# Projections of z, v and q by couples as seven block products, with more intermediates in DRAM and the last roots on ScalarE

## The chip, the cores and the metric

One core of a Trainium2 chip runs the kernel. The metric is the device time of one execution in microseconds; a profiled execution is shown by its span, which leaves out a little at both ends.

## The reference

One layer of an encoder block on x of 1024 tokens x 1024 features, float32:

```python
proj = h @ w_in                                    # 1024 x 2760
qkv, z, a, b, cq, ckv, k_rope = split(proj)
out_a = gated_deltanet(qkv, z, a, b, ...)          # conv of 4 taps + silu on q, k, v; chunked delta rule, 4 heads
out_b = mla(cq, ckv, k_rope, ...)                  # low-rank queries and keys, rotary key, block-causal softmax
h = layernorm(ALPHA * h + concat(out_a, out_b) @ w_out)
ffn = (silu(gate) * up) @ w_down                   # gate, up = causal conv of 3 taps over h @ w_up, 2 x 2816
ple = sigmoid(h @ w_gate + b) * (p @ w_proj)
out = layernorm(ALPHA * h + ffn + ple)
```

q, k, v, z are four tiles of 128 features each; the latent ckv has two and cq three; `rab` holds the rotary key and a, b. The causal convolution acts along the tokens, so a tile's second half of tokens needs the last three of its first half.

## The kernel before, in words

Every float32 product is made of three matmuls in TensorE's faster float32 format: operands are split into a high part (a copy on ScalarE) and a low part (a subtraction, mostly on DVE), and high x high, low x high and high x low are accumulated in PSUM. A projection tile is one job: `run_job` takes two halves of 512 tokens, each with `mm3` over 8 blocks of 128 features, so 48 matmuls of 128x512. `prepare_job` loads and splits a tile's weights two jobs ahead. Jobs run in the order rab, k0 to k3, v0 to v3, z0 to z3, q0 to q3, ckv, cq.

After a job `conv_half` runs the four taps (one ScalarE activation, three DVE operations that read PSUM) and a SiLU; `post_vq` and `post_z` store v, q and z to DRAM. Beside the projections run, as small generators: the gates (`gates`, ending in the `cum` matmuls), the decay matrices (`decay`, with `gg` products on POOL and DVE and `tp` matmuls), the squares and products of keys (`key_products`), the solve of 32 x 32 triangles on POOL (`solve`, 62 operations), the inverses (`inverse`, small matmuls), and the scan over eight chunks of tokens (`chunk`, `step`, `chunk_out`), which begins when v, q, z and all inverses are done. The remaining latent projections fill TensorE beside the scan. Then follow attention, the output projection, the FFN, and last `down_last`.

The order of TensorE, ScalarE, DVE and the SP queue in this part is written by a planner inside the program: each operation is booked with an assumed cost (`Engine`, a fixed time and a rate), generators yield until their inputs are booked as ready, and the order that results is pinned. POOL is booked but not pinned. Each engine then executes its list in order and waits for what it needs on the chip. Tiles come from pools with fixed counts of buffers (`s` 46, `gt` 17, `gp` 10, `raw`, `whi` and `wlo` 3 each).

The FFN up-projection, the gate and the down-projection already use seven products of half blocks in place of eight; z, v, q and the rest of `w_in` don't.

`down_last` ends the kernel: for each of eight rows of 128 tokens it adds the last products, forms mean and variance, and scales. Rows 0 to 6 take the inverse root on POOL (`inverse_root` with `e=pool`: a first guess by integer arithmetic and three Newton steps on 128x1), the last row on DVE; row 6 is finished by ScalarE and POOL.

Of the kernel before, what the change touches and what calls it, by code (L numbers as in the profile page):

```python
# [17 lines left out]
P = 128  # L18
# [20 lines left out]
ROWS = 1  # L39
RSD = 7  # L40
# [11 lines left out]
SOLVED = 15.0  # L52
# [19 lines left out]
def hybrid_block_kernel(  # L72
# [35 lines left out]
    busy, ready, used, writer = {}, {}, {}, {}  # L108
# [51 lines left out]
    class Engine:  # L160
# [5 lines left out]
        def __getattr__(self, name):  # L166
            f = getattr(self.engine, name)

            def call(*a, **k):
# [7 lines left out]
                if name == "dma_start":  # L177
                    end = book(self.engine, 0.5, 0.0, [], ins_ + outs)
# [10 lines left out]
    pool = Engine(nc.gpsimd, 0.15, 0.0019, False)  # L189

# [132 lines left out]
    matr = SR("matr", [P, 3, P])  # L323
# [13 lines left out]

    w_in_v = w_in[0].rearrange("(k p) f -> p k f", p=P)
    jobs = [("rab", [(O_KR, 64), (O_A, 8)])]
    jobs += [(f"k{h}", [((4 + h) * P, P)]) for h in range(NH)]  # L340
    jobs += [(f"v{h}", [((8 + h) * P, P)]) for h in range(NH)]
    jobs += [(f"z{h}", [(O_Z + h * P, P)]) for h in range(NH)]
    jobs += [(f"q{h}", [(h * P, P)]) for h in range(NH)]
    jobs += [(f"ckv{f}", [(O_CKV + f * P, P)]) for f in range(2)]
    jobs += [(f"cq{f}", [(O_CQ + f * P, P)]) for f in range(3)]
    w_of = [[] for _ in jobs]

    def prepare_job(j):
# [23 lines left out]

    xh = [[None, None] for _ in range(NKT)]
    xl = [[None, None] for _ in range(NKT)]

    def split_x(hf, k, ps):
        xh[k][hf], xl[k][hf] = SR(f"xh{k}{hf}"), SR(f"xl{k}{hf}")
        split(xh[k][hf], xl[k][hf], ps)

# [4 lines left out]
    for _ in range(8):  # L384
        mm(ps1[:, 0:P], junk, junk)
    def transpose_xq(i):
# [6 lines left out]
    def lower_half():  # L393
        yield wait(*xq[0])
        transpose_xq(0)
        for k in range(4):
            split_x(0, k, pieces[k])

# [10 lines left out]
    def second_half():  # L409
        yield wait(*xr)  # L410
        for k in range(NKT):
            ps = (B, G)[k % 2](f"xT1{k}")
# [29 lines left out]
    def run_job(j, post):  # L442
        ps = A(jobs[j][0])
        for hf in range(2):
            if hf == 0 and j + 2 < len(jobs) and j > 0:
                spawn(prepare_job(j + 2))
            run_half(j, ps, hf)
        for hf in range(2):
            post(hf, ps)
# [6 lines left out]
    krr = [S("krr0", [64, 512]), S("krr1", [64, 512])]  # L456
    abT = [S("abT0", [8, 512]), S("abT1", [8, 512])]
    done = set()

    def post_rab(hf, ps):  # L460
        c = slice(hf * 512, hf * 512 + 512)
        act.copy(abT[hf], ps[64:72, c])
        act.copy(krr[hf], ps[0:64, c])
# [41 lines left out]
    et_d = tc.dram_tile([NTB, P, 512], F32, name="et_d")  # L505
    qv_d = tc.dram_tile([3, NH, P, SEQ], F32, name="qv_d")
    l_d = tc.dram_tile([NTB, NH, P * P], F32, name="l_d")
    tb_d = tc.dram_tile([P, 1024], F32, name="tb_d")
    ub_d = tc.dram_tile([P, 1024], F32, name="ub_d")

# [13 lines left out]
    def conv_half(f, y, ps, hf, then):  # L524

        taps = [vec1[:, (3 - i) * 12 + f:(3 - i) * 12 + f + 1] for i in range(4)]
        act.activation(y, ps[:, hf * 512:hf * 512 + 512], AF.Identity, scale=taps[0])
        yield wait(y)
        for i in range(1, 4):
            lo_t = i if hf == 0 else 0  # L530
            d, s = y[:, lo_t:512], ps[:, hf * 512 + lo_t - i:hf * 512 + 512 - i]
            dve.scalar_tensor_tensor(d, s, taps[i], d, op0=ALU.mult, op1=ALU.add)
            yield wait(y)
        while "decay" not in done:
            yield 0.5
        act.activation(y, y, AF.Silu)
        yield wait(y)
        yield from then()
# [7 lines left out]
    flat = lambda v: v.rearrange("p t h -> p (t h)")  # L546

    def post_k(h):
        def post(hf, ps):
            def then():  # L550
                done.add(f"k{h}{hf}")
                yield 0
            spawn(conv_half(4 + h, kt[h][hf], ps, hf, then))
        return post

    l_pairs = [sbuf("gp", [P, 2, 512], f"l{j}") for j in range(NTB // 2)]
    lms = [l_pairs[t // 2][:, t % 2] for t in range(NTB)]
    ees = {}

    def decay(t):  # L560
        gg = [HR(f"gg{t}{i}") for i in range(2)]
# [3 lines left out]
        yield max(wait(*gg, maskr), room(tag))  # L565
# [4 lines left out]
        ees[t] = H(f"ee{t}")  # L570
        act.activation(ees[t], tp, AF.Exp)

    def decays():
# [3 lines left out]
        for t in range(NTB):  # L577
            spawn(decay(t), 1.3 * t)
        while len(ees) < NTB:
            yield 0.5  # L580
        done.add("decay")
        for t in range(NTB):
            yield max(wait(ees[t]), room("GB"[t % 2]))
            ep = (G, B)[t % 2](f"etp{t}")
            for h in range(NH):
                tr(ep[:, hs[h]], ees[t][:, hs[h]], ident)
            et = H(f"et{t}")
            act.copy(et, ep)
            yield wait(et)
            sync.dma_start(out=et_d[t], in_=et)  # L590
            yield 1.0
        done.add("decay_out")
        spawn(rotate_keys())

    def key_products():
        while not all(f"k{h}{hf}" in done for h in range(NH) for hf in range(2)):
            yield 0.5
        for t in range(NTB):
# [8 lines left out]
            yield wait(kd, kss)  # L607
            sync.dma_start(out=kd_d[t], in_=kd)
# [4 lines left out]
        for t in range(NTB):  # L613
            hf, c = blk[t]
            yield max(wait(bk), room("BG"[t % 2]))
            kkp = (B, G)[t % 2](f"kk_ps{t}")
            for h in range(NH):
                mm(kkp[:, hs[h]], kt[h][hf][:, c], kt[h][hf][:, c])
            lm, ee = lms[t], ees[t]
            for h in range(NH):  # L620
                dve.scalar_tensor_tensor(lm[:, hs[h]], kkp[:, hs[h]], bk[:, t, h:h + 1], ee[:, hs[h]], op0=ALU.mult, op1=ALU.mult)
            yield wait(lm)
            sync.dma_start(out=l_d[t].rearrange("h (p c) -> p h c", c=P), in_=heads(lm))
# [3 lines left out]

    whole = {}

    def solve():  # L630
# [8 lines left out]
        for j in range(31):  # L639
# [4 lines left out]
            pool.tensor_tensor(tb_[:, m:, 0:m], tb_[:, m:, 0:m], tv, op=ALU.subtract)  # L644
        yield wait(tb_)
# [4 lines left out]
        whole["tw"], whole["uw"] = [], []  # L650
        for hf in range(2):
            for name, d in (("tw", tb_d), ("uw", ub_d)):
                v = d.rearrange("(b i) (r s) -> (i r) b s", i=4, s=32)
                y = S(f"{name}{hf}", [P, 16, 32])
                sync.dma_start(out=y, in_=v[:, 16 * hf:16 * hf + 16])
                whole[name].append(y.rearrange("p (t h) s -> p t h s", h=NH))
        yield SOLVED
        for j in range(NTB // 2):
            yield from inverse(j)


    def inverse(j):

        u = l_pairs[j].rearrange("p t (h c) -> p t h c", c=P)
        tw, uw = (whole[n][j // 2][:, 2 * (j % 2):2 * (j % 2) + 2] for n in ("tw", "uw"))
# [6 lines left out]
        nw = H(f"nw{j}", [96, 2, NH, 32])  # L672
        for i in (0, 64):
            act.mul(nw[i:i + 32], pw[i:i + 32], -1.0)
        ti = H(f"ti{j}", [64, 2, NH, 64])
# [19 lines left out]
        nw2 = H(f"nw2{j}", [64, 2, NH, 64])  # L695
# [21 lines left out]
    chunks, states, outs = {}, [None], []  # L717

    def chunk(t):
# [3 lines left out]
        sync.dma_start(out=et, in_=et_d[t])  # L723
        sync.dma_start(out=kd, in_=kd_d[t])
        qc, vc = load_chunk("qc", 1, t), load_chunk("vc", 0, t)
        yield max(wait(qc, et), room("B", "G"))
        qk = B(f"qk_ps{t}")
        for h in range(NH):
            mm(qk[:, hs[h]], kt[h][hf][:, c], qc[:, hs[h]])
# [12 lines left out]
        chunks[t] = qc, et, vc, kd  # L742

    def step(t):

        hf, c = blk[t]
        while t not in chunks:
            yield 0.3
        qc, et, r, kd = chunks[t]
        state = states[t]  # L750
        if state is not None:
            yield max(wait(state, r), room("G"))
            ks = G(f"ks_ps{t}")
            for h in range(NH):
                mm(ks[:, hs[h]], kt[h][hf][:, c], state[:, hs[h]])
# [8 lines left out]
        if t < NTB - 1:  # L764
# [10 lines left out]
            states.append(new)  # L775
        spawn(chunk_out(t, qc, et, vn, state), 0.4)
# [38 lines left out]
    def scan():  # L815
        while not all(f"{n}{h}{hf}" in done for n in "vqz" for h in range(NH) for hf in range(2)) or "decay_out" not in done:
            yield 0.5
        yield wait(qv_d, et_d, kd_d)
# [3 lines left out]
        while not all(f"inverse{j}" in done for j in range(NTB // 2)):  # L822
            yield 0.5
# [3 lines left out]
    def post_vq(a, h, f):  # L827
        def post(hf, ps):
            y = S(f"{'vq'[a]}{h}_{hf}")
            def then():  # L830
                sync.dma_start(out=qv_d[a, h, :, hf * 512:hf * 512 + 512], in_=y)
                yield 0
                done.add(f"{'vq'[a]}{h}{hf}")
            spawn(conv_half(f, y, ps, hf, then))
        return post

    def post_z(h):
        def post(hf, ps):
            y = S(f"z{h}_{hf}")
            act.activation(y, ps[:, hf * 512:hf * 512 + 512], AF.Silu)  # L840
            sync.dma_start(out=qv_d[2, h, :, hf * 512:hf * 512 + 512], in_=y)
# [1120 lines left out]
```

## Time and profile before

| | |
|---|---|
| runs (3) | median 1372.06 us (1371.88 to 1374.73) |
| profiled execution | 1371.56 us, span 1369.7 us |
| granted TensorE clock, mean | 0.992 |
| PE busy | 1333.5 us (97%), 7185 matmuls |
| DVE busy | 986.3 us (72%) |
| ScalarE busy | 626.6 us (46%) |
| POOL busy | 189.2 us (14%) |

Busy matmul time is modelled and counts the pipeline, so matmuls overlap in it: what one costs in a stream is read from the distance of their starts. Stretches are given in microseconds from the span's start.

### The profile page before, as it was taken

The page shows a single profiled execution, that of the slowest core. Times are in us where ns is not written, and L with a number is a line of the kernel's source. Part 1 is how long each engine was busy: PE and PEld are TensorE (multiplying, and loading weights), DVE is VectorE, ACT ScalarE, POOL GpSimd, SP SyncE. Part 2 cuts the span into 40 slices and gives each one's busy share as a digit, 9 for nine tenths or more (in the row PEclk, how much of TensorE's full clock was granted, in tenths as well). Part 3 has the DMA queues.
Part 4 walks back from the last instruction along what each step waited for, and adds up shares of the span by engine and source line. Part 5 has one row for each costly group of instructions (what it writes and reads, how often), then busy time and mean ns, then how long its engine had stood idle before and what let it go on. Part 6 is the DMA issues. An engine that isn't in the chain of part 4 may idle for free.

```text
span 1369.7 us, 19833 instructions
## 1 busy us (share of the span) xinstructions
PE 1333.5 (97%) x7185; PEld 1127.6 (82%) x7185; DVE 986.3 (72%) x1781; ACT 626.6 (46%) x1213; POOL 189.2 (14%) x418
## 2 busy tenths in 40 slices
PE   9999999999989999999999999999999999999995
PEld 6788887789878988888998888888888888888884
DVE  3746224365467795777889888888888887988857
ACT  3544123555335572246435555555555554444511
POOL 0341450144420000230000000000000000000036
PEclk9999999999999999999999999999999999999998
DMA  7034535445431243336452221222212249406112
GB/s 219 24 119 151 139 100 132 140 121 146 108 114 58 81 127 107 120 108 214 148 162 78 85 85 63 92 93 77 92 64 91 93 164 361 160 22 205 51 44 94
DMA packets 181089, 159.19 MB, mean 116 GB/s; under 512 B 26138, under 2 KB 140672, under 8 KB 180992
## 3 DMA queue, kind: packets, MB, share of 16 engines
q1 hardware_dynamic: 180784, 157.67, 37.0%
q8 instruction: 56, 0.92, 0.3%
q14 instruction: 41, 0.34, 0.1%
q10 hardware_dynamic: 144, 0.26, 0.1%
q0 software_dynamic: 64, 0.00, 0.0%
HBM read 117.53 MB, written 39.85 MB: 115 GB/s over the span
## 4 chain that ended last, share of the span: by engine, by line
PE 54%; DVE 3%; POOL 2%; issue 1%; ACT 1%; DMA 1%; SPq 0%; DVEq 0%; ACTq 0%; POOLq 0%
PE ffX L199 17%; PE ffZ L199 9%; PE dX L199 7%; PE dP L199 5%; PE ffY L199 4%; PE gX L199 3%; PE mixp L199 3%; PE gY0P L199 1%; PE gY1P L199 1%; POOL rs_u L170 1%; DVE h L170 1%; PE dl L199 1%; POOL ln_v L170 1%; DMA mix_raw<-mm_d 1%; POOL ln_rs L170 0%
## 5 line engine op out<-in xcount | busy, mean ns | idle before, releaser
L170 POOL TENSOR_SCALAR ln_v<-ln_ss 128x1 f32<-128x1 f32 x7 | 9.0, 1285 | 710.6 <-ACT sink L170 710.1
L199 PE MATMUL dX<-dP,dP 128*128 128x512 f32 x432 | 99.5, 390 | 0.0
L199 PEld LDWEIGHTS dX<-dP,dP 128*128 128x128 f32 x432 | 81.1, 188 | 17.0 <-DVE h L170 0.2
L170 DVE SCALAR_TENSOR_TENSOR gate<-c,vec,gate 128x511 f32<-128x511 f32 (+1 forms) x132 | 69.8, 571 | 11.4 <-ACT gate L170 10.7
L199 PE MATMUL dP<-dP,dP 128*128 128x512 f32 x324 | 75.4, 391 | 0.0
L199 PEld LDWEIGHTS dP<-dP,dP 128*128 128x128 f32 x324 | 60.6, 188 | 13.3 <-DVE h L170 0.9
L170 ACT CAST dP<-b 128x512 fp32r<-128x512 f32 x45 | 28.0, 622 | 60.4 <-issue 20.8
L170 ACT COPY c<-ffX 128x512 f32<-128x512 f32 x44 | 25.8, 586 | 38.4 <-PE ffX L199 38.4
L170 ACT ACTIVATE gate<-c,vec 128x512 f32<-128x512 f32 x44 | 35.9, 817 | 14.8 <-DVE c L170 12.8
L170 DVE SCALAR_TENSOR_TENSOR u<-ffX,vec,u 128x511 f32<-128x511 f32 (+1 forms) x88 | 40.2, 478 | 0.1
L170 DVE SCALAR_TENSOR_TENSOR u<-c,vec,u 128x511 f32<-128x511 f32 (+1 forms) x44 | 33.0, 751 | 7.1 <-ACT u L170 6.3
L170 ACT ACTIVATE p<-s,mx,q_f 128x128 f32<-128x128 f32 (+7 forms) x32 | 26.7, 835 | 24.8 <-DVE mx L170 21.1
L170 DVE TENSOR_TENSOR dP<-b,dP 128x512 fp32r<-128x512 f32 x45 | 31.0, 690 | 8.5 <-ACT dP L170 8.4
L170 ACT ACTIVATE gate<-gate 128x512 f32<-128x512 f32 x44 | 27.6, 627 | 12.1 <-DVE gate L170 12.1
L199 PE MATMUL ov<-pth,v 128*128 128x256 f32 x160 | 31.3, 287 | 0.1
L170 DVE TENSOR_TENSOR dP<-a,dP 128x512 fp32r<-128x512 f32 x45 | 31.0, 688 | 0.0
L170 DVE TENSOR_TENSOR ptl<-pt,pth 128x512 fp32r<-128x512 f32 (+1 forms) x40 | 24.8, 633 | 7.9 <-ACT pth L170 7.8
L170 DVE TENSOR_TENSOR u<-u,gate 128x512 f32<-128x512 f32 x44 | 30.2, 686 | 0.0
L170 DVE SCALAR_TENSOR_TENSOR kt<-k,vec,kt 128x512 f32<-128x512 f32 (+3 forms) x24 | 16.4, 740 | 19.0 <-ACT kt L170 19.0
L170 ACT CAST dP<-a 128x512 fp32r<-128x512 f32 x45 | 27.7, 617 | 5.1 <-issue 2.2
L170 POOL TENSOR_TENSOR h<-h,b 128x1024 f32<-128x1024 f32 x8 | 19.3, 2414 | 76.4 <-DVE h L170 75.1
L170 ACT ACTIVATE u<-ffX,vec 128x512 f32<-128x512 f32 x22 | 17.2, 780 | 23.1 <-PE ffX L199 23.1
(1373 smaller groups left out, 4179.5 us busy)
## 6 DMA issues: line engine op xcount, KB each, us to landing
wup<-in_ffn_w_up_dram SPq DMA_DIRECT2D x88, 256.0 KB
b<-in_ffn_w_down_dram SPq DMA_DIRECT2D x54, 256.0 KB
a<-g_d SPq DMA_DIRECT2D x45, 256.0 KB
g_d<-u SPq DMA_DIRECT2D x44, 256.0 KB
wgP_raw<-in_ple_w_gate_dram SPq DMA_DIRECT2D x16, 512.0 KB
wo_raw<-in_w_out_dram SPq DMA_DIRECT2D x8, 512.0 KB
xres<-in_x_dram SPq DMA_DIRECT2D x8, 512.0 KB
pp_d<-pp SPq DMA_DIRECT2D x16, 256.0 KB
```

Source lines behind the costliest of these rows:

```text
L170: ins = f(*a, **k)
L199: on_pe(nc.tensor.matmul(o, a, b, start=start, stop=stop, **k_), max((k - 1.0) * a.shape[-1] / 1900.0, n * k / 2370.0), o, a, b)
```

## The change

1. The 12 tiles of z, v and q are taken in six couples, z0 with z1 to q2 with q3. With the two tiles as blocks of columns, the two halves of the features as blocks of the sum and the two halves of the tokens, each couple is a 2 x 2 block product that is computed with seven products of 12 matmuls instead of eight. The four sums of weights per couple run on POOL; the sums of blocks of x (T1 to T4) are made once, by ScalarE copies and 24 POOL operations, and split like the others.

```diff
+    couples = [("z0", "z1"), ("z2", "z3"), ("v0", "v1"), ("v2", "v3"), ("q0", "q1"), ("q2", "q3")]
+    TERMS = {"P1": ("X", "B11"), "P2": ("Y", "B21"), "P5": ("Y", "T1"), "P6": ("X", "T2"), "P3": ("Y", "B22"), "P7": ("X", "T3"), "P4": ("X", "T4")}
...
+    def pair_operand(n):
...
+        act.copy(w[:, 0], src)
+        yield wait(w)
+        dve.tensor_tensor(w[:, 1], src, f32(w[:, 0]), op=ALU.subtract)
+        d[name] = w
+        if name == "P2":
...
+            pool.tensor_tensor(a21, a11, a21, op=ALU.subtract)
+            pool.tensor_tensor(d["s"], a22, a21, op=ALU.subtract)
+            pool.tensor_tensor(a11, d["s"], a11, op=ALU.add)
+            pool.tensor_tensor(a12, a12, d["s"], op=ALU.subtract)
+
+    def pair_operands():
+        for n in range(len(seq)):
+            while n > place[0] + 3:
+                yield 0.3
...
+        for k in range(4):
+            until(lambda: xb[block][k] is not None)
+            h, l = xb[block][k]
+            for i, (a, b) in enumerate(((0, h), (1, h), (0, l))):
+                settle(w, b)
+                mm(ps, w[:, a, k], b, start=first and k == i == 0, stop=k == 3 and i == 2, skip_group_check=not first)
```

2. The block results are combined with one ScalarE copy and one DVE addition each (`pair_after`), except the last; the taps of a tile then read SBUF (three halves of a couple) or PSUM (one), and the first three tokens of the second half are completed by three short operations (`conv_edge`). At most two tiles of v or q are in their convolution at a time.

3. More waits in DRAM: the keys after SiLU (`qv_d` gets a fourth part, and each chunk loads its own), the decay matrices with their transposes (`ee_d`), the key products until the inverse, and the split x of features 0 to 511, tokens 512 to 1023 (`b12_d`, read again for ckv and cq). Key products begin when all decays are done. The solve yields between its steps; an inverse is made per pair of chunks, and a step of the scan waits only for its own. The planner's assumed costs of ScalarE and DVE are larger in this part:

```diff
+    usual = {e: (e.fixed, e.rate) for e in (act, dve)}
+    act.fixed, act.rate, dve.fixed, dve.rate = 0.2, 0.00078, 0.16, 0.00105
...
-        while t not in chunks:
+        while t not in chunks or f"inverse{t // 2}" not in done:
...
             pool.tensor_tensor(tb_[:, m:, 0:m], tb_[:, m:, 0:m], tv, op=ALU.subtract)
+            yield 1.2
```

4. In `down_last` all roots go to ScalarE, with the first guess on DVE; all rows but the last are finished by one DVE operation.

```diff
+        def root(v, scale):
+
+            h, y = T("ln_v", 1), T("ln_rs", 1)
+            act.activation(h, v, AF.Identity, scale=-0.5 * scale, bias=eps)
+            dve.tensor_scalar(y.bitcast(I32), h.bitcast(I32), -0.5, float(0x5F3759DF - 2 ** 22 - 2 ** 30), op0=ALU.mult, op1=ALU.add)
+            for _ in range(3):
+                u, w, z = T("rs_u", 1), T("o_ms", NH)[:, 0:1], T("ln_rs", 1)
+                act.activation(u, y, AF.Identity, scale=h)
+                act.activation(w, u, AF.Identity, scale=y, bias=three)
+                act.activation(z, w, AF.Identity, scale=y)
+                y = z
+            return y
...
         def finish_row(t):
-            if t < NTB - 1 - ROWS:
-                dve.scalar_tensor_tensor(acc[t], acc[t], rss[t], b, op0=ALU.mult, op1=ALU.add)
-            else:
-                act.mul(acc[t], acc[t], rss[t])
-                pool.tensor_tensor(acc[t], acc[t], b, op=ALU.add)
+            dve.scalar_tensor_tensor(acc[t], acc[t], rss[t], b, op0=ALU.mult, op1=ALU.add)
```

## Rows read from the trace of the kernel before

**Rows 1.** The page: chain of waits, and gigabytes per second in 40 slices.

```profile
PE 54%; DVE 3%; POOL 2%; issue 1%; ACT 1%; DMA 1%; SPq 0%; DVEq 0%; ACTq 0%; POOLq 0%
...
GB/s 219 24 119 151 139 100 132 140 121 146 108 114 58 81 127 107 120 108 214 148 162 78 85 85 63 92 93 77 92 64 91 93 164 361 160 22 205 51 44 94
```

**Rows 2.** Timeline, projections: start, duration, engine, line, operation, count.

```profile
85.33 1.98 PE L199 MATMUL v<-xh,v_hi 128*128 128x512 f32 x8
87.14 1.98 PE L199 MATMUL v<-xh,v_lo 128*128 128x512 f32 x8
...
227.85 0.39 PE L199 MATMUL ckv<-xh,ckv_hi 128*128 128x512 f32 x1
```

**Rows 3.** Windows: stretch, length, PE, PEld, DVE, ACT, POOL, clock, DMA, GB/s.

```profile
85.30:227.90 142.60, 142.60 (x706) 118.98 (x704) 60.58 (x100) 45.42 (x114) 54.67 (x94) 1.00 0.47 126
153.00:194.00 41.00, 41.00 (x183) 33.97 (x182) 5.33 (x4) 7.23 (x10) 36.04 (x62) 1.00 0.40 112
...
900.00:1000.00 100.00, 100.00 (x443) 82.87 (x442) 86.48 (x150) 51.49 (x83) 0.00 (x0) 1.00 0.27 84
```

**Rows 4.** Groups of DVE by form: shapes, count, busy, mean ns, idle before.

```profile
L170 DVE TENSOR_TENSOR dP<-b,dP 128x512 fp32r<-128x512 f32 x45 | 31.0, 690 | 8.5 <-ACT dP L170 8.4
L170 DVE SCALAR_TENSOR_TENSOR u<-c,vec,u 128x511 f32<-128x511 f32 x22 | 16.5, 751 | 6.3 <-ACT u L170 6.3
...
L170 DVE SCALAR_TENSOR_TENSOR l<-kk_ps,gs,ee 128x128 f32<-128x128 f32 x32 | 9.0, 344 | 6.6 <-POOL tb__1376 L170 3.4 <-PE kk_ps L199 3.1
L170 DVE SCALAR_TENSOR_TENSOR v<-v,vec,v 128x512 f32<-128x512 f32 x12 | 8.9, 743 | 0.0
...
L170 DVE TENSOR_TENSOR v_lo<-v_raw,v_hi 128x1024 fp32r<-128x1024 f32 x4 | 4.9, 1219 | 0.6 <-ACT v_hi L170 0.6
```

**Rows 5.** Groups of POOL by form, the first 300 us.

```profile
L170 POOL TENSOR_TENSOR gg<-mats,g_hi 128x512 fp32r<-128x512 f32 x8 | 10.4, 1326 | 18.3 <-DVE g_hi L170 18.3
```

**Rows 6.** Timeline of POOL and of DVE, decays.

```profile
43.42 10.37 POOL L170 TENSOR_TENSOR gg<-mats,g_hi 128x512 fp32r<-128x512 f32 x8 [18.31 <-DVE g_hi L170]
...
45.44 1.58 DVE L170 TENSOR_TENSOR gg<-mats,g_lo 128x512 fp32r<-128x512 f32 x1
...
48.25 1.21 DVE L170 TENSOR_TENSOR gg<-mats,g_lo 128x512 fp32r<-128x512 f32 x1
49.38 2.06 DVE L170 TENSOR_TENSOR k_lo<-k_raw,k_hi 128x1024 fp32r<-128x1024 f32 x1
...
52.02 0.87 DVE L170 TENSOR_TENSOR gg<-mats,g_lo 128x512 fp32r<-128x512 f32 x1
...
53.47 3.27 DVE L170 TENSOR_TENSOR gg<-mats,g_lo 128x512 fp32r<-128x512 f32 x5
```

**Rows 7.** Timeline of DVE and of POOL, rotation of queries.

```profile
377.39 1.67 DVE L170 TENSOR_TENSOR qm<-qm,qm 128x512 f32<-128x512 f32 x1
...
378.59 1.62 POOL L170 TENSOR_TENSOR qm<-qm,qm 128x512 f32<-128x512 f32 x1
```

**Rows 8.** Timeline of PE, gates.

```profile
43.57 0.75 PE L199 MATMUL cum<-gs,mats 128*128 128x32 f32 x6
```

**Rows 9.** Timeline of PE, DVE and POOL at the end; ScalarE's smallest operation, scan.

```profile
1353.87 0.28 PE L199 MATMUL dl<-wl,gh 128*128 128x256 f32 x1
...
1354.14 1.28 DVE L170 SCALAR_TENSOR_TENSOR h<-h,ln_rs,b 128x1024 f32<-128x1024 f32 x1 [1.49 <-POOL ln_rs L170]
...
1358.78 0.41 DVE L170 TENSOR_TENSOR h<-dl,h 128x256 f32<-128x256 f32 x1
...
1361.20 2.29 DVE L170 SCALAR_TENSOR_TENSOR ln_rs<-rs_u,ln_rs 128x1 f32<-128x1 f32 x1
...
1365.08 1.41 DVE L170 SCALAR_TENSOR_TENSOR h<-h,ln_rs,b 128x512 f32<-128x512 f32 x2
...
1360.96 2.52 POOL L170 TENSOR_TENSOR h<-h,b 128x1024 f32<-128x1024 f32 x1 [1.26 <-ACT h L170]
...
249.04 0.20 ACT L170 ACTIVATE junk<-junk 128x1 f32<-128x1 f32 x1
```

More of the change, by code (lines that the diff above doesn't have):

```diff
@@ L509, in hybrid_block_kernel @@
     ub_d = tc.dram_tile([P, 1024], F32, name="ub_d")
+    drams.update(key(x[:]) for x in (kd_d, ee_d, qv_d, l_d))
     def heads(ap):
@@ L534, in conv_half, with conv_taker, take, halves @@
         while "decay" not in done:
             yield 0.5
-        act.activation(y, y, AF.Silu)
+        act.activation(y, src, AF.Silu)
         yield wait(y)
-        yield from then()
+    live = set()
+    def conv_taker(f_of, out_of, then):
+        ys = {}
+        def take(name, role, hf, c):
+            f = f_of(name)
+            def halves():
+                if name not in ys:
+                    while name[0] != "k" and len(live) > 1:
+                        yield 0.3
+                    if name not in ys:
+                        if name[0] != "k":
+                            live.add(name)
+                        ys[name] = out_of(name)
+                y = ys[name]
+                yield from conv(f, y[hf], c[hf])
+                if role == "a" and hf == 1:
+                    conv_edge(f, y[1], c[0])
+                    done.add(f"conv {name}")
+                if role == "b" and hf == 0:
+                    conv_edge(f, y[1], c[0])
+                    done.add(f"conv {name}")
+                for i in {("a", 0): (0,), ("a", 1): (1,), ("b", 1): (), ("b", 0): (0, 1)}[role, hf]:
+                    yield from silu(y[i], y[i])
+                    then(name, i, y[i])
+                    if (role, i) in (("a", 1), ("b", 1)):
+                        live.discard(name)
+            spawn(halves())
+        return take
@@ L564, in decay @@
         tag = "BG"[t % 2]
-        yield max(wait(*gg, maskr), room(tag))
+        yield max(wait(whole, maskr), room(tag))
         tp = (B, G)[t % 2](f"tp{t}")
@@ L569, in decay @@
             mm(tp, utrir, y, start=False, stop=i == 1)
-        ees[t] = H(f"ee{t}")
-        act.activation(ees[t], tp, AF.Exp)
+        ees[t] = sbuf("gp", [P, 2, 512], f"ee{t}")
+        act.activation(ees[t][:, 0], tp, AF.Exp)
+        yield max(wait(ees[t]), room("GB"[t % 2]))
+        ep = (G, B)[t % 2](f"etp{t}")
+        for h in range(NH):
+            tr(ep[:, hs[h]], ees[t][:, 0, hs[h]], ident)
+        act.copy(ees[t][:, 1], ep)
+        yield wait(ees[t])
+        sync.dma_start(out=ee_d[t], in_=ees[t])
+        done.add(f"decay{t}")
     def decays():
@@ L577, in decays, with put, load_decays @@
         for t in range(NTB):
-            spawn(decay(t), 1.3 * t)
-        while len(ees) < NTB:
-            yield 0.5
-        done.add("decay")
[L582 to L592, printed above, removed]
-        spawn(rotate_keys())
+            spawn(decay(t))
+            while t > 1 and f"decay{t - 2}" not in done:
+                yield 0.2
+        while not all(f"decay{t}" in done for t in range(NTB)):
+            yield 0.2
+        done.add("decay")
+        spawn(rotate_keys())
+    def put(kd, t):
+        yield wait(kd)
+        sync.dma_start(out=kd_d[t], in_=kd)
+    def load_decays(j):
+        y = sbuf("gp", [P, 2, 512], f"lm{j}")
+        sync.dma_start(out=y, in_=ee_d[2 * j:2 * j + 2, :, 0].rearrange("t p c -> p t c"))
+        return y
     def key_products():
-        while not all(f"k{h}{hf}" in done for h in range(NH) for hf in range(2)):
+        while not all(f"k{h}{hf}" in done for h in range(NH) for hf in range(2)) or "decay" not in done:
             yield 0.5
@@ L775, in step @@
             states.append(new)
+        done.add(f"step{t}")
         spawn(chunk_out(t, qc, et, vn, state), 0.4)
@@ L815, in scan @@
     def scan():
-        while not all(f"{n}{h}{hf}" in done for n in "vqz" for h in range(NH) for hf in range(2)) or "decay_out" not in done:
+        while not all(f"{n}{h}{hf}" in done for n in "vqz" for h in range(NH) for hf in range(2)) or "projected" not in done:
             yield 0.5
-        yield wait(qv_d, et_d, kd_d)
+        yield wait(qv_d, ee_d, kd_d)
         act.activation(junk[:, 0:1], junk[:, 0:1], AF.Exp)
@@ L821, in scan, with out_pair, keep, take_z @@
         spawn(chunk(1), 2.0)
-        while not all(f"inverse{j}" in done for j in range(NTB // 2)):
-            yield 0.5
         for t in range(NTB):
             yield from step(t)
[L827 to L841, printed above, removed]
-            done.add(f"z{h}{hf}")
-        return post
+    def out_pair(name):
+        y = sbuf("gp", [P, 2, 512], f"{name}_out")
+        return y[:, 0], y[:, 1]
+    def keep(name, hf, y):
+        sync.dma_start(out=qv_d["vqz".index(name[0]), int(name[1]), :, hf * 512:hf * 512 + 512], in_=y)
+        done.add(f"{name}{hf}")
+    takers["v"] = conv_taker(lambda name: 8 + int(name[1]), out_pair, keep)
+    takers["q"] = conv_taker(lambda name: int(name[1]), out_pair, keep)
+    def take_z(name, role, hf, c):
+        y = c[hf]
+        if role == "b" and hf == 0:
+            y = H(f"{name}_{hf}")
+            act.copy(y, c[hf])
+        def gate():
+            yield from silu(y, y)
+            keep(name, hf, y)
+        spawn(gate())
+    takers["z"] = take_z
     raws, tot = {}, {}
@@ L1035, in value_pair @@
         for t2 in range(NTB // 2):
+            if h == 0:
+                until(lambda: f"step{2 * t2 + 1}" in done)
             ps = (B, G)[t2 % 2](f"v_{h}_{t2}", [P, 2, 256])
```

422 lines of the change are left out of this document (281 added, 141 removed).

## The prediction

> **What bounds the kernel now.** I read the chain of waits on the page first: TensorE holds 54% of it, with a POOL entry for the small tiles `rs_u`, `ln_v`, `ln_rs` that can only come from the last layer norm [rows 1]. Then TensorE in order of time over the projections: the reader is to see groups of eight 128x512 matmuls that follow each other at 1.81 us without a gap, from the first v (85.33) to the first ckv matmul (227.85) [rows 2]. The busy times of that stretch agree: PE 142.6 of 142.6 us, DVE 60.6, POOL 54.7 [rows 3]. So until 228 us TensorE's count of matmuls sets the time. In the last 16 us another thing does: the last matmul ends at 1354.15, while DVE was until 1354.14 waiting for POOL's `ln_rs` and ends 11 us later [rows 9].
>
> **Removed matmuls.** Before, 12 tiles cost 2 halves x 8 x 3 = 48 matmuls each, 576. After, 6 couples cost 7 products x 4 x 3 = 84 each, 504. One is 1.81 / 8 = 0.2266 us [rows 2], so 72 x 0.2266 = **-16.3 us** if nothing else becomes late. The stretch would shrink from 142.5 to 126.2 us.
>
> **What must fit beside it on DVE.** Durations are those of rows 4: 0.69 for a two-tensor operation of 128x512, 0.75 for a convolution tap, 0.344 for a 128x128 step of the key products, 0.74 for a tap from PSUM. A couple needs 7 low parts and 3 additions, 6.9 us; a v or q couple also 12 taps (9.0) and 6 short edges, which I put at 0.15 each, 16.8 us. Two z couples are 13.8, four v/q couples 67.2; nine low parts of the sums of x 6.2, the last key tile's taps 4.4, `kd` 5.5, key products 32 x 0.344 = 11.0. Together 108.1 of 126.2 us, a slack of 18. That load alone is bearable: in the FFN, which is made of the same seven products, DVE is busy 86% while PE has no gap [rows 3].
>
> **What it shares with POOL.** The change puts 24 sums of weights on POOL in this stage, beside nine operations of the key rotation and the 62 of the solve (36.0 us [rows 3]). A 128x512 sum takes POOL about 1.3 us [rows 5], so 24 x 1.3 + 9 x 1.3 + 36 = 79 us. When POOL and DVE work on SBUF tensors at the same time they lengthen each other. Where POOL ran 8 such operations in 10.37 us, three `gg` of DVE took 1.58, 1.21 and 0.87 against 0.65 undisturbed, and `k_lo` 2.06 against 1.22 [rows 4, 6]: 2.5 us lost, 0.25 per us of POOL. Where both run nothing but such operations, one of DVE takes 1.67 instead of 0.65 beside one of 1.62 on POOL [rows 7]: 0.63 per us. Lower end: 0.25 x 79 = 20, less the slack, +2 us. Upper end: 0.63 on the 57 us that lie beside v and q couples and 0.25 on the other 22, 41 less 18, +23 us. What DVE loses beyond its slack goes to TensorE, since the low part of each operand is queued on DVE behind the taps and is made only three products (8 us) ahead. I take **+10**: DVE's mix here, with additions and some taps from PSUM, is nearer to rows 6, and some of the solve will fall behind the projections.
>
> The Trainium skill, page "SBUF — State Buffer", section "Who interferes with whom", speaks against the change here: a DVE instruction with two SBUF inputs and a GpSimd instruction that reads SBUF exclude each other, and the second waits for the whole of the first. The lengths in rows 6, 7 and 9 agree. By that rule alone the sum takes the third rival's term below in place of +10.
>
> **The start.** 24 sums of x go to POOL from about 15 us, when the lower blocks are split: 24 x 1.3 = 31 us, until 46. POOL is now idle until 43.42, when the first `gg` of the decays runs [rows 6], and `cum` on TensorE waits for the gates at 43.57 [rows 8]. The gates' own small two-tensor operations on DVE run in those microseconds, and DVE also gets seven low parts (4.8 us). Bounds: 0 if other k matmuls stand ahead of `cum` and the first `tp`, +5 if the whole overlap turns into a wait. I take **+3**: 46.4 - 43.4.
>
> **Edits that I put at nothing.** Eight extra ScalarE copies at the start, the block copies and splits later: ScalarE is busy 45 of 142.6 us [rows 3], and about 40 us more still fits; it is tight (by the same count some 45 of 49 us) only beside the z couples and the key squares. Stores and loads of keys, decays, x: some 6 MB more in 126 us, 48 GB/s on top of 126 [rows 3]; the page has slices above 300 [rows 1]. They also stand in SP's queue ahead of weight loads, and a store that waits for a late SiLU holds the next weights; with a lead of 8 us this costs only when DVE is late already. The inverse, scan and latent projections keep their matmuls; the scan may start as soon as one inverse is done, while the first values wait for its steps (their `gp` buffers) and have their weights prepared later than now. For the waits around all these I take 0, bounds -4 to +4.
>
> **The end.** Before: the last pair of `h` operations starts at 1365.08, 10.9 us after the last matmul, because finishing row 5 waited for POOL, so DVE takes the last 256 columns only at 1358.78; a step of the root then takes 2.29 us beside POOL's `h<-h,b` of 2.52 [rows 9]. After: no POOL work. DVE needs per row 2 x 0.65 + 1.3 + 1.3 + 0.2 = 4.1 us, and PE 24 x 0.2266 = 5.4, so DVE keeps up. From the last matmul: addition, statistics and aggregate 1.2, ScalarE's `h` 0.3, first guess on DVE 0.2 = 1.7. Then DVE has row 6 (1.3) and two halves (1.4), until 4.4, and ScalarE nine operations of 128x1 at 0.20 [rows 9], 3.6; if each dependent step costs 0.30, 4.5. The last pair starts at 4.5 instead of 10.9: **-6.4** (bounds -4 to -7).
>
> **Sum.** The profiled execution took 1371.56 (span 1369.7 and 1.9 around it): 1371.56 - 16.3 + 10 + 3 - 6.4 = 1361.9. The median of the runs is 0.5 above that execution: 1362.
>
> **Rivals.**
> - *Everything is covered.* POOL's sums fall beside DVE's PSUM work and PE keeps its 0.2266: 1371.56 - 16.3 - 6.4 + 0.5 = 1349. For it: the FFN's gapless TensorE at 86% DVE. Against: no POOL work lies beside the FFN.
> - *DVE and POOL alternate (the slower side).* Place: v and q couples while the solve runs. Price 0.63 on all POOL work there, plus late convolutions that hold PSUM: +36 when the slack of 18 is already used by the key products sliding out of the z couples; 1371.56 - 22.7 + 3 + 36 + 0.5 = 1388. It decides from 0.48 lost per us of POOL on (0.48 x 79 - 18 = 20 eats both gains). For: rows 7. Against: rows 6.
> - *The shared access itself is full.* DVE's two-SBUF operations, 14 + 28 + 9 low parts at 0.69 and 36 taps at 0.75, are 62 us; with POOL's 79 that is 141 in 126.2 us: +15, 1371.56 - 22.7 + 3 + 15 + 0.5 = 1367. This is the rule of the Trainium skill named above.
> - *The solve ends late.* It ran from 153 to 194; if shared POOL time moves its end by over 25 us while projections end 16 us earlier, latent projections run out before the scan does: +8 on the forecast, 1370.
> - *The roots on ScalarE don't shorten the end* (each step over 0.4 us): only POOL's block on DVE goes, 2.3 us; 1366.
>
> **How the numbers follow.** Forecast 0.38 (own range 1355 to 1368); covered 0.24; full access 0.12; alternation 0.18; late solve 0.04; end not shorter 0.04. 0.2% is 2.7 us, about what a measurement of this kernel tells from no change. Faster: 0.38 + 0.24 + 0.06 + 0.04 = 0.72; same: the rest of the full access and the late solve with a share of the alternation, 0.09; slower 0.19. The range 1348 to 1380 leaves out half of the alternation and a few hundredths below.
>
> **What would show it.** Right: 504 matmuls in the couples at 0.227, DVE above 85% beside v and q, low parts of 1 us and more while POOL runs, gaps before products that end on DVE or POOL, a last pair 4 to 5 us after the last matmul. Wrong: couples without gaps beside the solve (then 1349), or gaps of over 20 us in sum. The end is wrong if a ScalarE step takes over 0.3 us.

## The result, and the profile after

| | median of the runs | range | profiled execution |
|---|---|---|---|
| before | 1371.97 us | 1371.44 to 1374.73 (4 runs) | 1371.56, span 1369.7 |
| after | 1436.03 us | 1434.58 to 1438.35 (4 runs) | 1436.09, span 1434.3 |

The change makes the kernel slower, 1.046 times the time before (95% interval 1.0445 to 1.0475), 64 us; the forecast was 1362 us, 10 us faster. Landmarks on TensorE, us from the start of the span:

| | before | after | stage, after minus before |
|---|---|---|---|
| `cum` starts | 43.57 | 51.89 | |
| last matmul of the k tiles ends | 85.3 | 103.9 | +18.6 |
| first `ckv` matmul | 227.85 | 303.2 | +56.8 |
| first `kn` matmul | 362.05 | 431.5 | -5.9 |
| last `dl` matmul starts | 1353.87 | 1423.2 | |
| last pair of `h` operations starts, after that matmul | 11.2 | 6.5 | -4.7 |

The loss lies in two stages: the start, and above all the couples, the stage that was to shrink by 16.3 us and grow by 10. The page of the kernel after, its TensorE and clock slices and the chain, which answers to [rows 1] (there 54% PE, 1% ACT):

```profile
PE   8786877799998999999999999999999999999996
...
PEclk9987999999999999999999999999999999999999
...
PE 71%; DVE 5%; ACT 5%; issue 2%; DMA 1%; POOL 1%; SPq 0%; DVEq 0%; ACTq 0%; POOLq 0%
```

A slice is 36 us: TensorE is no longer full in the first eight. The windows of the same kernel (stretch, length, then busy time of PE, PEld, DVE, ACT, POOL, granted clock, DMA share, GB/s) answer to the first line of [rows 3], where PE was busy 142.60 of 142.60:

```profile
30.00:40.00 10.00, 8.56 (x30) 4.33 (x29) 3.06 (x6) 3.98 (x9) 9.69 (x11) 0.83 0.48 126
...
100.00:120.00 20.00, 12.34 (x42) 8.73 (x41) 14.52 (x23) 10.17 (x19) 9.90 (x8) 0.83 0.09 33
103.90:303.20 199.30, 151.04 (x682) 112.15 (x681) 113.73 (x183) 78.65 (x182) 81.64 (x112) 0.91 0.39 116
303.20:431.50 128.30, 124.54 (x1077) 108.52 (x1076) 65.77 (x142) 69.83 (x229) 40.12 (x141) 1.00 0.62 166
```

In 199.3 us TensorE is busy 151, and part of that at the lower of its two clock levels, 1.2 and 2.4 GHz (mean granted clock 0.91, before 1.00). DVE is busy 114 of 199 us: it is not full. What TensorE waited for in the couples (engine, line, releaser: sum in us, times, longest):

```profile
PE pair L198 <- DVE c L167: 17.6, 17, 3.0
PE pair L198 <- ACT c L167: 17.0, 17, 5.2
PE pair L198 <- ACT win4P L167: 6.1, 1, 6.1
PE pair L198 <- DVE win0P L167: 2.5, 1, 2.5
PE pair L198 <- ACT win0P L167: 2.4, 1, 2.4
```

34 waits are for `c`, the copies and additions that take a product out of PSUM. The third couple in order of time: the first matmuls of its products, answering to [rows 2], and below, from DVE and ScalarE, what each waited for.

```profile
190.19 0.73 PE L198 MATMUL pair<-xh,win2P 128*128 128x512 f32 x2 [0.67 <-ACT c L167]
...
193.99 0.74 PE L198 MATMUL pair<-xT2h,win2P 128*128 128x512 f32 x2 [0.78 <-DVE c L167]
...
197.72 0.73 PE L198 MATMUL pair<-xT1h,win2P 128*128 128x512 f32 x2 [0.68 <-ACT c L167]
...
201.41 0.73 PE L198 MATMUL pair<-xT3h,win2P 128*128 128x512 f32 x2 [0.68 <-ACT c L167]
```

```profile
193.24 0.69 DVE L167 TENSOR_TENSOR c<-pair,c 128x512 f32<-128x512 f32 x1 [1.86 <-PE pair L198]
...
197.08 0.58 ACT L167 COPY c<-pair 128x512 f32<-128x512 f32 x1 [1.88 <-PE pair L198]
...
200.78 0.58 ACT L167 COPY c<-pair 128x512 f32<-128x512 f32 x1 [2.06 <-PE pair L198]
```

The product that starts at 193.99 (`xT2h`, P6) adds to X. What it waits for, the addition from 193.24 to 193.93, reads Y, which P2 has just finished. The next one writes Y and waits for the copy of X. A product takes 3.7 us where twelve matmuls at 0.2266 take 2.72: the wait and some 0.25 us around it, 1.0 us each time.

### The profile page after: what moved, and what is told of

It reads as the page before. It is cut to its first block, busy times and chain, and to the rows that moved or that the text cites. A ratio compares the mean times of both kernels' runs of the same rounds, so it can differ in the third digit from the quotient of the medians.

```text
span 1434.3 us, 20071 instructions
## 1 busy us (share of the span) xinstructions
PE 1344.6 (94%) x7113; PEld 1121.9 (78%) x7113; DVE 1046.2 (73%) x1882; ACT 687.1 (48%) x1366; POOL 223.7 (16%) x389
## 4 chain that ended last, share of the span: by engine, by line
PE 71%; DVE 5%; ACT 5%; issue 2%; DMA 1%; POOL 1%; SPq 0%; DVEq 0%; ACTq 0%; POOLq 0%
PE ffX L198 17%; PE ffZ L198 8%; PE dX L198 7%; PE dP L198 5%; PE ffY L198 4%; PE mixp L198 4%; PE pair L198 4%; PE gX L198 3%; PE s L198 3%; PE cq L198 2%; PE ov L198 2%; PE ckv L198 2%; PE gY0P L198 1%; PE gY1P L198 1%; PE v L198 1%
## 5 line engine op out<-in xcount | busy, mean ns | idle before, releaser
L167 DVE TENSOR_TENSOR c<-pair,c 128x512 f32<-128x512 f32 x18 | 12.4, 690 | 35.0 <-PE pair L198 31.7
L167 ACT ACTIVATE p<-s,mx,q_f 128x128 f32<-128x128 f32 (+7 forms) x32 | 26.7, 834 | 22.3 <-DVE mx L167 18.6
L167 DVE SCALAR_TENSOR_TENSOR kt<-k,vec,kt 128x511 f32<-128x511 f32 (+5 forms) x36 | 19.0, 563 | 24.3 <-ACT kt L167 24.0
L167 ACT ACTIVATE c<-c 128x512 f32<-128x512 f32 x22 | 13.6, 630 | 30.9 <-DVE c L167 30.9
```

The lines of the kernel that those rows point to most:

```text
L167: ins = f(*a, **k)
```

## The experiments

Each was run in three rounds beside the kernel before; ratios are to it, with 95% intervals. The base of the later ones is the third.

| run | edit | us | ratio |
|---|---|---|---|
| e1 | X and Y in PSUM tiles of their own | 1404.31 | 1.0226 [1.0209, 1.0243] |
| e2 | splits of the sums of x after the decays | 1409.1 | 1.0253 [1.0228, 1.0278] |
| e3 | both | 1394.35 | 1.015 [1.0133, 1.0167] |
| e4 | the kernel before with the new end alone | 1369.21 | 0.9966 [0.9953, 0.9979] |
| e5 | e3, sums of weights on DVE | 1397.39 | 1.0175 [1.0153, 1.0197] |
| e6 | e3 without the solve's operations | 1382.06 | 1.0063 [1.0048, 1.0078] |
| e7 | e3, first couple earlier, sums of x after the gates | 1405.2 | 1.0227 [1.0207, 1.0247] |
| e8 | e5 and e7 | 1420.38 | 1.0343 [1.0327, 1.0358] |
| e9 | e3, z couples beside the solve | 1400.01 | 1.0197 [1.0175, 1.0219] |
| e10 | e3 without the sums of x | 1376.28 | 1.0023 [1.0014, 1.0032] |
| e11 | e10 and e6 | 1363.13 | 0.9922 [0.9906, 0.9939] |
| e12 | e9, copies of x by POOL | 1416.41 | 1.0311 [1.0278, 1.0344] |

**e1, X and Y apart.**

```diff
-                until(lambda: f"conv {last}" in done)
-            y = A(f"pair{f}")
-            d["X"], d["Y"] = y[:, 0:512], y[:, 512:1024]
...
+            d[bank_] = A(f"pair{bank_}{f}")[:, 0:512]
...
+            d["C21"] = H(f"c21_{f}")
+            act.copy(d["C21"], d["X"])
```

> The changed kernel, with the two chains X and Y of a couple in two PSUM tiles instead of two halves of one, and the last X copied out at once. Theory A (the shared tile makes each product wait until the one before it is taken out of PSUM): products follow each other at 2.7 instead of 3.7 to 3.9 us, the 34 us of waits for the copies and additions c nearly vanish (one per couple stays), the couples lose 35 to 50 us and the kernel comes to about 1390 to 1400. Theory B (my prediction: DVE and POOL hold each other up): the waits only move to the operands, less than 10 us are gained, 1426 or more.

-31.7 us. The same copies and additions are there, and one copy more in each couple of v and q, but the third couple of e1 runs through (its products start 2.72 us apart, with nothing named before them):

```profile
175.38 0.62 PE L198 MATMUL pairY<-xh,win2P 128*128 128x512 f32 x2
...
178.10 0.62 PE L198 MATMUL pairX<-xT2h,win2P 128*128 128x512 f32 x2
...
180.82 0.62 PE L198 MATMUL pairY<-xT1h,win2P 128*128 128x512 f32 x2
```

In the couples of e1 the waits for `c` are 2.5 us instead of 34.6. The couples lose 29.8 us (169.5 instead of 199.3) and not 35 to 50, as other waits take part of the place: those for the operands `win3P` to `win5P` rise from 8.9 to 16.0 us, and one of 4.7 for the taps of the last key tile (`kt`) comes up. The edit does one thing beside the tiles: with the last X copied out, a couple no longer waits for a convolution that still reads PSUM (the `until` above). No wait of a couple's matmul in the kernel after is for such taps, so this isn't where the 34.6 us were. So the order was kept by the tile and not by what its halves hold. The Trainium skill ("PSUM — Partial Sum Buffer", section "PSUM bank collisions raise a hardware error") asks for semaphores by bank and quadrant; X and Y are 2 KB per partition each, and here the waits went by the tile, wider than that rule.

**e2, late splits, and e3, both.**

```diff
-        yield 5.0
+        while "decay" not in done:
+            yield 0.5
         for name, m in [("T2", m) for m in range(4)] + [("T1", m) for m in range(3)]:
```

> The changed kernel, with the splits of the sums T2 and T1 of x begun only when the decays are done. Theory A (the splits fill ScalarE's and DVE's lists in front of the decays and the taps of the keys, which delays the end of the keys from 85 to 104 us): the keys end 10 to 15 us earlier, 1421 to 1426, if the first couple doesn't wait for the sums instead. Theory B (POOL's sums of x hold the gates, or the decays two at a time are slow by themselves): the keys end no more than 4 us earlier.

> Both edits together. If both theories A hold: the sum of the two gains, about 1375 to 1385. If the first couple waits for the late sums: no better than the split tiles alone.

e2 gives -27 us, more than expected. In the profiled executions, 24.2 us apart, 12.2 lie before the end of the k tiles (91.7 instead of 103.9), 7.3 in the couples and 4.9 between the first `ckv` and the first `kn` matmul. The first couple waits for its own operands as before (2.4 and 2.8 us), but the longest wait for `c` falls from 5.2 to 2.1. In the kernel after, ScalarE and DVE, which work through their lists in order, show why (ScalarE's casts wait for DVE's low parts, and the first `exp` of the decays, `ee<-tp`, stands behind them until 65.14):

```profile
53.81 0.62 ACT L167 CAST xT1h<-xT 128x512 fp32r<-128x512 f32 x1 [5.31 <-DVE xT2l L167]
...
57.66 0.62 ACT L167 CAST xT1h<-xT 128x512 fp32r<-128x512 f32 x1 [3.07 <-DVE xT2l L167]
...
62.52 0.62 ACT L167 CAST xT1h<-xT 128x512 fp32r<-128x512 f32 x1 [4.24 <-DVE xT1l L167]
...
65.14 0.59 ACT L167 ACTIVATE ee<-tp 128x512 f32<-128x512 f32 x1
```

e3 missed its 1375 to 1385. The two gains overlap: 32 and 27 alone, 42 together. Part of both is the same, as the traces read: the long waits for `c` of the first couple, and the low clock with them (from 120 to 160 us 0.74 and 0.83 in the kernel after, 0.88 and 1.00 in e1, 0.87 and 1.00 in e2).

**e4, the new end alone** (the layer norm's tail of the kernel after, put into the kernel before; everything else is before).

> The kernel before, with only its last part taken from the changed kernel (roots on ScalarE, rows finished on DVE). The end after the last matmul took 15.6 us before and 10.8 after the change, so 4.5 to 5 us less, 1367. If the gain came from elsewhere than these lines: within 1 us of 1372.

0.34% faster by the ratio, 4.7 us (interval 2.9 to 6.5), over 10 runs against 13. This is the one part of the change that pays, and the version to keep.

**e5, sums of weights on DVE; e6, no solve.** What e3 still waits for in the couples, and what e6 does:

```diff
-            pool.tensor_tensor(a21, a11, a21, op=ALU.subtract)
+            dve.tensor_tensor(a21, a11, a21, op=ALU.subtract)
...
-            pool.tensor_tensor(tv, lb[:, m:, j:j + 1].broadcast_to([P, n, m]),
-                                    tb_[:, j:j + 1, 0:m].broadcast_to([P, n, m]), op=ALU.mult)
-            pool.tensor_tensor(tb_[:, m:, 0:m], tb_[:, m:, 0:m], tv, op=ALU.subtract)
```

> The kernel with X and Y in tiles of their own and late sums of x (1394), and the four sums of weights of each couple on DVE instead of POOL. What it still loses beside the solve are waits of TensorE for the operands of the third and fourth couple: 8.3 us for a ScalarE cast, 4.7, 1.4 and 1.3 for DVE's low parts. Theory Q (the sums stand in POOL's list between the 62 operations of the solve: the second sum of a couple started 12 us after the first): these waits go, the operands come in time, 1380 to 1386. Theory L (POOL and DVE lengthen each other, as the prediction had it at +10): the sums leave POOL but add 0.7 to 1.1 us each to a DVE that is busy 18.2 to 18.7 of 20 us there; taps stay at 1.0 to 1.1 us and the waits move to DVE: 1390 to 1398.

> The same base (1394) with the 62 operations of the solve on POOL left out (its table stays the identity, so the inverse is not computed; its loads, stores and the rest stay). Both theories of the loss beside the solve agree that it goes, so this measures its size, which the prediction put at +10: waits for operands of the third and fourth couple at 0 to 2 us in place of 15, taps of DVE at 0.75 us in place of 1.0 to 1.1, and 1375 to 1383. A third theory, that ScalarE's copies are the limit of a couple: still over 1388. The scan may also start earlier or later by a few us.

Waits of TensorE, first e3, then e6:

```profile
PE pairX L198 <- ACT win4P L167: 8.3, 1, 8.3
PE pairX L198 <- DVE win3P L167: 4.7, 1, 4.7
PE pairY L198 <- DVE kt L167: 4.6, 1, 4.6
```

```profile
PE pairY L198 <- DVE kt L167: 5.7, 1, 5.7
PE pairY L198 <- ACT win5P L167: 3.9, 1, 3.9
...
PE pairX L198 <- DVE win4P L167: 2.2, 1, 2.2
...
PE pairX L198 <- DVE win3P L167: 0.7, 1, 0.7
```

Without the solve the kernel is 12.3 us shorter. Taking the sums off POOL gave nothing (+3.0): DVE, busy 18.7 of 20 us from 180 to 200 in e3, is busy 19.7 there in e5. That speaks for theory L, DVE lengthened by POOL, and against the late place in POOL's list as the whole story. One product shows both. In e3 the second sum of the fifth couple's weights (`win_s`) starts at 213.07, 13.5 us after the first, with the solve in between, and its cast on ScalarE at 218.70, behind a SiLU that waited for DVE's taps. In e5 the same sum is done at 209.95, and the product still starts only at 218.67, after 5.3 us of waiting for DVE's low part. DVE's line in e3 while the solve runs, and then in e6 without it:

```profile
191.82 1.12 DVE L167 SCALAR_TENSOR_TENSOR v_out<-c,vec,v_out 128x511 f32<-128x511 f32 x1
192.87 1.17 DVE L167 TENSOR_TENSOR win3P<-win,win3P 128x512 fp32r<-128x512 f32 x1
...
199.24 0.69 DVE L167 TENSOR_TENSOR c<-pairX,c 128x512 f32<-128x512 f32 x1
```

```profile
189.40 0.75 DVE L167 SCALAR_TENSOR_TENSOR v_out<-c,vec,v_out 128x511 f32<-128x511 f32 x1
190.06 0.69 DVE L167 TENSOR_TENSOR win3P<-win,win3P 128x512 fp32r<-128x512 f32 x1
```

Beside the solve taps and low parts take 1.1 us for the 0.75 and 0.69 of [rows 4] and of e6; the addition that reads PSUM keeps its 0.69.

**e7 and e8, the first couple earlier.**

```diff
-            if hf == 0 and j == 4:
+            if hf == 0 and j == 3:
                 load_pair(0, 0)
...
+                    act.copy(c[hf], ps[:, hf * 512:hf * 512 + 512])
...
+        while "gates" not in done:
+            yield 0.5
...
-                pool.tensor_tensor(low[o, m], low[a, m], low[b, m], op=ALU.subtract)
+            later.append((m, sums))
```

> The same base (1394) with three edits at the first couple: the 24 sums of x on POOL begin after the gates, the weights of the first couple are loaded and its first two operands split one key tile earlier, and the last key tile is copied out of PSUM by ScalarE before its taps, so that Y's tile is free. It tells what is left of the start: TensorE now waits 2.4 and 2.5 us for the first couple's operands, 4.6 for the taps of the last key tile, and works at 0.80 of its clock from 100 to 120 us. If these are late operands and a late tile, they go and with them the low clock: 1377 to 1384. If DVE's list there (late low parts of the sums of x) is the limit, another wait takes their place: 1390 to 1396.

> The edits of both: sums of weights on DVE and the early first couple. If the two losses are independent, the gains add: 1365 to 1375. If DVE's list is full, the early operands and the sums displace each other and it stays at 1380 to 1392.

Both missed: +10.9 and +26.0. The sums didn't move behind the gates: the planner doesn't pin POOL's order, and in the trace they ran without a pause from 25.9 to 56.7, over the whole of the gates, so `cum` came at 59.2. In e8 the first couple waits 8.9 us in two pieces for its last low part of x (5.6 in e7, where the weights' sums are on POOL). e8 is 8.5 us behind e3 at the first `kn` matmul, and the rest of the 26 is lost after it. There the scan runs on into attention: its last transposes (`oT_ps`) start at 438.6, in e3 at 396.4. Why the scan ends so late was not taken apart by a run.

**e9, the z couples beside the solve.**

```diff
-    couples = [("z0", "z1"), ("z2", "z3"), ("v0", "v1"), ("v2", "v3"), ("q0", "q1"), ("q2", "q3")]
+    couples = [("v0", "v1"), ("v2", "v3"), ("q0", "q1"), ("z0", "z1"), ("z2", "z3"), ("q2", "q3")]
```

> The base with X and Y apart and late sums (1394), the couples in another order: v, v, q, z, z, q in place of z, z, v, v, q, q, so that the two z couples, which put no convolution on DVE (6.9 us of it per 19 us of TensorE instead of 16.8), stand where the solve runs on POOL. Theory L (the loss beside the solve is DVE lengthened by POOL): the 15 us of waits for operands of the third and fourth couple shrink to 0 to 5, and 1380 to 1388. Theory Q (the sums of weights are late in POOL's list): the waits stay, 1390 to 1398. Against both: v couples then stand beside the key products and the last splits of x, which may cost 3 to 8 us at the first couple.

The first `ckv` matmul comes 4 us earlier (258.9 for 262.9), and the waits for operands of the fourth and fifth couple (`win3P`, `win4P`) fall from 14.3 to 7.8 us, but DVE is now busy 19.9 of 20 us from 140 to 160, and what is gained is lost again after the couples (the scan's last transposes start at 410.4 instead of 396.4): 1400, outside what either theory expected. It doesn't tell the theories apart.

**e10, no sums of x; e11, also no solve.**

```diff
-            y = low[name, m] = S(f"x{name}{m}")
-            act.copy(y, ps)
...
+        for n, b in (("T1", "B11"), ("T2", "B21"), ("T3", "B22"), ("T4", "B11")):
+            xb[n] = xb[b]
```

> The base (1394) without the sums of x: no copies of x by ScalarE at the start, no sums on POOL, no splits; the products of T1 to T4 read blocks of x that are there already, so the products have the same matmuls and wrong values. It measures what the sums of x cost from the first transposes to the last couple. Theory S (the start's loss is these sums: transposes that wait 0.5 to 1.2 us for ScalarE's copies, TensorE then at 0.5 to 0.8 of its clock from 30 to 40 us, and 128x32 operations of the gates that take 0.8 to 1.06 us beside POOL instead of 0.18): cum back at 43.5 to 45 from 53.5, the k tiles end at 85 to 87 instead of 92, waits at the first couple (2.4, 2.5, 4.6) shrink; 1378 to 1386. Rival: the start's loss is the extra decay stores and key stores on the queues: cum stays above 50, 1390 or more.

> Both left out, the sums of x and the 62 operations of the solve: what the seven products would give with POOL nearly free. If the two losses add (12 from the solve, 8 to 16 from the sums), 1364 to 1374. If the products without POOL's company ran gapless, as my rival of full cover had it, the first ckv matmul would come at 212 to 215 and the time be 1352 to 1356. If it stays above 1374, the limit left is DVE's own load beside v and q.

e10 is 18.1 us under e3, a little more than expected, half of it before the couples (the k tiles end at 82.7 instead of 91.9), half within them (162 instead of 171 us). e11 is 31.2 under e3, and 12.3 + 18.1 = 30.4: the two add. In e11 the stage of the couples still takes 150 us where its work is 126.2:

```profile
84.30:234.27 149.97, 137.53 (x714) 110.88 (x713) 102.55 (x175) 76.80 (x179) 43.59 (x52) 0.97 0.54 156
```

12.4 us of that are waits for operands and copies that ScalarE and DVE make for the couples themselves (the largest 2.4 and 2.2). The rest is lower clock (mean 0.97), restarts after the waits, and work that moved: 112 of the small matmuls of the inverses lie in this stage, before the change 32. How much each of these is worth was not measured.

**e12, copies of x by POOL.**

```diff
-            act.copy(y, ps)
+            pool.tensor_tensor(y, f32(xh[k][1]), f32(xl[k][1]), op=ALU.add)
```

> The order of couples of the run with z beside the solve, and the copies of the second half of x made by POOL from the parts (high plus low) instead of by ScalarE from PSUM: eight more operations on POOL (10 us), none on ScalarE, and PSUM is free sooner. If ScalarE's copies hold the transposes, the waits of 0.5 to 1.2 us and the low clock from 30 to 40 us go and the rab tile ends at 34 to 36 instead of 41.4; the gates then run wholly beside POOL and take some 14 us instead of 8. Together 0 to 5 us less than the same kernel without it.

Half right: the copies do hold the transposes, but the price is on the other side, and the kernel takes 16.4 us more than e9. First the kernel after, where transposes wait for ScalarE's copies (which had themselves waited 0.76 to 0.81 us for DVE's low part of the same PSUM tile) and `rab` then runs at 0.43 us per matmul; then e12, where `rab` ends at 34.2 (as before: 33.9) and `cum` comes at 56.3:

```profile
29.02 0.59 ACT L167 COPY xT<-xT 128x512 f32<-128x512 f32 x1 [0.76 <-DVE xl L167]
...
29.66 0.65 PE L201 MATMUL xT<-ident,xr 128*128 128x128 f32 x4 [1.17 <-ACT xT L167]
...
32.72 0.63 PE L198 MATMUL rab<-xh,rab_hi 128*72 128x512 f32 x1
33.15 0.63 PE L198 MATMUL rab<-xl,rab_hi 128*72 128x512 f32 x1
...
51.89 0.86 PE L198 MATMUL cum<-gs,mats 128*128 128x32 f32 x6
```

```profile
34.00 0.39 PE L198 MATMUL rab<-xh,rab_lo 128*72 128x512 f32 x1
...
56.32 1.49 PE L198 MATMUL cum<-gs,mats 128*128 128x32 f32 x6 [9.99 <-DVE gs L167]
```

The gates on DVE, in the kernel before, where POOL is idle, and in e12, where it runs sums of 1.25 us:

```profile
38.76 0.35 DVE L170 RECIPROCAL gs<-gs 128x32 f32<-128x32 f32 x1
...
40.04 0.18 DVE L170 TENSOR_SCALAR gs<-gs 128x32 f32<-128x32 f32 x1
40.26 0.19 DVE L170 TENSOR_TENSOR gs<-gs 128x32 f32<-128x32 f32 x1
```

```profile
41.30 0.35 DVE L167 RECIPROCAL gs<-gs 128x32 f32<-128x32 f32 x1
...
46.31 1.18 DVE L167 TENSOR_SCALAR gs<-gs 128x32 f32<-128x32 f32 x1
47.52 1.20 DVE L167 TENSOR_TENSOR gs<-gs 128x32 f32<-128x32 f32 x1
```

Most operations of 0.19 us take 1.2, about one operation of POOL; the reciprocal isn't touched, and from 52.4 to 55.4 every second one keeps its 0.19. The chain of the gates takes 19 us instead of 6, TensorE waits 10 us for it, and its granted clock from 50 to 60 us is 0.54. The Trainium skill ("SBUF — State Buffer", section "Who interferes with whom") says that the second of the two waits for the whole of the first, and that `tensor_scalar` can take the shared ports too; the trace agrees with both.

## Why the prediction was wrong

The failed step is the one called "Edits that I put at nothing", in its part on the block copies. I counted how many copies fit on ScalarE by its busy time, and they do fit: it is busy 78.65 of 199.3 us. What I didn't ask is who waits for each copy. X and Y of a couple are two halves of one PSUM tile, so that nearly every product waits for the copy or the addition of the one ahead (34 of 42 by name), 1.0 us each where its operands are there. The runs put this at 31.7 us (e1), half of the 64 us lost. My own sign of being wrong, gaps of over 20 us in sum, shows: TensorE is idle for 48 of the 199.3 us. I had the line that says it (`d["X"], d["Y"] = y[:, 0:512], y[:, 512:1024]`) and named no wait for it.

Point by point:

- *Removed matmuls, -16.3.* The count holds: e11's groups have 48 matmuls of X and 36 of Y in each of six couples, 504, and they follow at 0.2266 us where nothing waits (e1's fence). The gain never reached the end: in no run, not even in e11, were the couples shorter than the 142.5 us before.
- *DVE and POOL, +10.* Right in mechanism and near in size: e6 puts what the solve costs beside the couples at 12.3. (e6 takes away the lengthening of DVE and the solve's places in POOL's list at once; e5 speaks for the first.) I had looked for it on DVE's load and gaps in front of products, and there it is (`win3P`, `win4P`). It is not what made the kernel slow.
- *The start, +3.* Mis-sized: +18.6 until the k tiles end. Of that 12.2 are the splits of T2 and T1, queued on ScalarE and DVE ahead of the decays and the key taps (e2: 103.9 to 91.7); I had counted the seven low parts as 4.8 us of DVE and not as places in two lists. 9.2 are the copies and sums of x (e10: 91.9 to 82.7, which is 2.6 earlier than before): the transposes wait for ScalarE's copies, TensorE works in part at its lower clock level from 30 to 40 us (0.83 in the window), and the gates run beside POOL. `cum` is 8.3 us late: 5.7 because the gates begin after a late `rab` (43.07 instead of 37.41), 2.7 because their chain takes longer. The upper bound of +5 rested on POOL's end at 46, and POOL does end at 48.0; what I missed is that the eight copies I put at nothing delay `rab` and that most small operations of the gates wait for a whole one of POOL while it runs. [rows 6 and 7] are of long operations, and I used their rate.
- *Stores, loads and the scan, 0.* No loss, and a gain a little beyond the bound of -4: from the first `ckv` to the first `kn` matmul 5.9 us less (e11: 9.0). I had named the cause that fits, the scan starting after one inverse, and not counted on it; no run tests it. Part of it is no gain: 80 of the inverses' small matmuls lie in the couples' stage now, before 32.
- *The end, -6.4.* -4.7 by the trace and -4.7 by e4, inside its bounds, but by my own sign (a step over 0.3 us) the steps were wrong. The nine ScalarE steps and the pieces before them, answering to [rows 9]:

```profile
1423.19 0.28 PE L198 MATMUL dl<-wl,gh 128*128 128x256 f32 x1
...
1425.66 0.26 DVE L167 BATCH_NORM_AGGREGATE ln_mv<-ln_st 128x2 f32<-128x24 f32 x1
...
1426.47 0.29 ACT L167 ACTIVATE rs_u<-ln_rs,ln_v 128x1 f32<-128x1 f32 x1 [0.22 <-DVE ln_rs L167]
1426.80 0.39 ACT L167 ACTIVATE o_ms<-rs_u,gs,ln_rs 128x1 f32<-128x1 f32 x1
1427.22 0.29 ACT L167 ACTIVATE ln_rs<-o_ms,ln_rs 128x1 f32<-128x1 f32 x1
...
1429.69 1.42 DVE L167 SCALAR_TENSOR_TENSOR h<-h,ln_rs,b 128x512 f32<-128x512 f32 x2 [0.74 <-ACT ln_rs L167]
```

  The statistics end 2.45 us after the last matmul (1423.47 to 1425.92) and not 1.2, as DVE, which had centred row 6 until then, still has three column pieces to do; the nine steps start 0.33 to 0.42 us apart, 3.2 in all, where I took 0.20 to 0.30 (and added up 0.1 too much: 1.7 + 9 x 0.30 is 4.4).

The sum of the runs: 1436.0 - 31.7 (one tile, e1) - 10.0 (late splits, e3) - 18.1 (sums of x, e10) - 13.2 (solve, e11) = 1363. My forecast without its own +10 and +3 was 1349; the 14 us between are about e11's couples, 24 us over their work, less the 9 of the scan. That rest was only read from waits and not taken apart by a run. Of the rivals the alternation of DVE and POOL pointed to the right side with the wrong cause: its price is the 12 of e6. No rival had the wait between two products.

## What to carry to other kernels

When results move from one accumulation to several short ones, ask of each copy out of PSUM not whether its engine has time but which matmul is next and whether that writes the same tile; give two accumulations two tiles. Small operations of a chain (the gates in e12) can lose a whole operation of the neighbour each, so a helper's work on POOL belongs where DVE runs long operations from PSUM (the addition that kept its 0.69 us), or nothing on the path. An edit that adds work to two in-order lists is priced by its place in them, not by its sum.

## What the runs showed of the hardware

In e12 most DVE operations of 128x32 with 0.18 to 0.19 us took 1.13 to 1.23 us beside POOL sums of 1.25 us, while POOL's own durations stayed (four sums beside the gates in 4.99 us, from 43.67 on; a single one before them 1.29); RECIPROCAL kept 0.35 us. Two accumulations in the two halves of one PSUM tile waited 0.67 to 0.78 us at each product for the copy or addition that read the other half, and ran through in two tiles (e1). A dependent ScalarE step of 128x1 took 0.29 us, with one more operand per partition 0.39 us, against 0.20 for the one in [rows 9]; the Trainium skill ("ScalarE: Activation LUTs", section "What ACT_TABLE_LOAD costs") gives some 280 ns with a 128x1 bias and 93 ns for each such operand more, and the trace agrees.
